# Two decoder blocks in split fp32: the down projections move into the braided stage's slots and banks

## The chip, the cores and the metric

The kernel runs on one core of one Trainium2 chip. The metric is device time in microseconds (us) for one execution, 2815.57 us as the median of 3 runs (2812.67 to 2816.57).

## The reference

Two transformer blocks run one after the other on 256 tokens of width 2048 in fp32. Cut to the matrix products:

```python
# first block
proj = rmsnorm(x) @ w_in                       # queries, keys, pool, gates
y_pool, y_attn = pool(proj) @ w_pool_o, attention(proj) @ w_attn_o
x = x + (g_pool * y_pool + g_attn * y_attn) @ w_out
h2 = rmsnorm(x)
x = x + (silu(h2 @ w_ffn_gate) * (h2 @ w_ffn_up)) @ w_ffn_down      # 2048 -> 5632 -> 2048
# second block
proj = rms_norm(x) @ w_in_2                    # stick-breaking attention, spatial gating
x = x + (sigmoid(ga) * y_a + sigmoid(gb) * y_b) @ w_out_2
h2 = rms_norm(x)
x = x + square(relu(h2 @ w_ff1_2)) @ w_ff2_2                        # 2048 -> 8192 -> 2048
```

## The kernel before

Every matrix product keeps fp32 accuracy by splitting each operand into a high part and a low part in `fp32r`: `x*w` is taken as `xh*wh + xh*wl + xl*wh`, three matmuls. The activations are stationary (128 x 128), the weights move (512 or 256 columns).

**Pieces.** The weights come in pieces of 512 KB. A piece is loaded by SyncE's DMA queue (SP) into a raw buffer (`R`, 4 buffers, or `G`, 3 buffers, for Strassen pieces). ScalarE (ACT) rounds it to the high part, a CAST (line L226). VectorE (DVE) subtracts to get the low part (L228). Both go into a slot of the tile `W`. Then TensorE (PE) multiplies. An ordinary piece is 1024 numbers wide and feeds 12 matmuls of 512 columns (L258 with the high part, L259 with the low part, L260 with the high part). A Strassen piece is four blocks of 256 columns, to which DVE first adds three sums (L203 to L205). It is 1792 wide when split and feeds 21 matmuls of 256 columns (L310 to L312).

**Kinds of piece.** There are three: `PLAIN`, `MIX` and `STR`. `W` has 13 x 1024 columns, and the kinds share them. A PLAIN piece takes one of six slots, 0 to 5. A MIX piece takes one of slots 0 to 2. A STR piece takes one of two wide slots that lie on the columns of PLAIN slots 3 to 5. So PLAIN slots meet the columns of both other kinds, and MIX and STR never meet. Slots of one kind are used in turn.

**Order.** All engines' instructions are written out in one order by `drive()`, which walks over a list of jobs. Before the matmuls of piece k it emits the splits of the pieces up to k + 4 (PLAIN) or k + 3 (MIX, STR), but only while the slot's last user has been emitted already (`free_h[...] <= used[0]`). Where that doesn't hold, this split and all behind it come later in the queues of ACT and DVE, behind whatever was emitted in between. Engines work their queues in order. On the chip a split also waits until the slot's last user has left PE.

**Stages.** The work around the change, for each of the two feed-forward parts:

- `wide(...)`: the product with `w_out` or `w_out_2`, four chunks of 512 columns with 8 PLAIN pieces each. After each chunk the sum into `X` (L860) and squares (L404) are taken, and one piece into the next chunk the result is transposed by PE (`transposed_s`, L352) and split for the next stage.
- the braided stage: `braid(...)` weaves a MIX chunk (gate, or an even chunk of `w_ff1_2`) with a Strassen chunk (up, or an odd chunk). The MIX chunk sums in banks 4 and 5 of PSUM, the Strassen chunk in banks 0 to 3. At the end of a braid `fin` of `strassen` reads banks 0 to 3 (ACT L323, DVE L324 to L327), and in the second block ACT then applies relu and square (L1182, L1183). The first block has 4, 4 and 3 braids in its three groups, the second block 2 braids in each of four groups.
- the down stage after each group: four chunks with `w_ffn_down` (8, 8 and 6 PLAIN pieces each) or `w_ff2_2` (8 each), into banks taken in turn from `FREE[PLAIN]`, 0 to 3. They are added to `X` by DVE (L896). Into the first of the four chunks the transposes of the last braid's result are put (`transposed`, PE L382, then ACT L369 and DVE L370 copy them out of PSUM). These use auxiliary banks: 4, 5, 6 and 7 in mode PLAIN, 6 and 7 in mode MIX. The second block transposes two chunks at once there (`two`), which takes four banks' worth.

`stage(MIX)` and `stage(PLAIN)` only set which auxiliary banks are used. There are three sorts of change of stage: from `wide` to the first braid, from the last braid of a group to the down stage, and from the down stage to the next group's first braid.

Of the kernel before, what the change touches and what calls it, by code (L numbers as in the profile page):

```python
# [17 lines left out]
NT = 2  # L18
D = 2048
KT = D // P  # L20
# [6 lines left out]
PLAIN, MIX, STR = 0, 1, 2  # L27
# [44 lines left out]
def body(tc, d, out):  # L72
# [4 lines left out]
    with tc.manual_schedule(), \  # L77
# [48 lines left out]

        mode = [PLAIN]
        naux = [0]
        FREE = {PLAIN: [0, 1, 2, 3], MIX: [4, 5]}
        AUX = {PLAIN: (4, 5, 6, 7), MIX: (6, 7)}  # L130

        def bank_at(b):
# [14 lines left out]
        def stage(m):  # L147
            run(lambda: mode.__setitem__(0, m))

        def hslots(kind, n):  # L150

            if kind == STR:
                return (n % 2) * 1792, (2 + n % 2) * 1792, 1792
            s = n % (3 if kind == MIX else 6)
            o = 7168 + 1024 * s if s < 3 else 1024 * (s - 3)
            return o, o + 3072, 1024

        def drive():
            pcs = [j for j in jobs if j[0] == "pc"]
# [2 lines left out]
            seen_h, seen_r, cnt = {}, {}, {}  # L162
            for i, j in enumerate(pcs):
                kind = j[5]
                n = cnt.get(kind, 0)
                cnt[kind] = n + 1
                num.append(n)
                a, b, w = hslots(kind, n)
                cells = [(o + x) // 256 for o in (a, b) for x in range(0, w, 256)]
                free_h.append(max(seen_h.get(x, -1) for x in cells))  # L170
                seen_h.update((x, i) for x in cells)
                rk = kind == STR
                m = cnt.get(("r", rk), 0)
# [34 lines left out]
            def split(upto):  # L208
                while ns[0] <= min(upto, len(pcs) - 1) and free_h[ns[0]] <= used[0]:
                    i = ns[0]  # L210
                    dma()
                    if i in before_split:
                        before_split[i]()
                    sums(i + 2)
                    kind = pcs[i][5]
                    a, b, w = hslots(kind, num[i])
# [42 lines left out]
            pe.matmul(o, x[0], w[1], start=False, stop=False)  # L259
            pe.matmul(o, x[1], w[0], start=False, stop=last)  # L260

        def chunk(pair, w, kts, c0, n, evict, row0=0, inject=None, kind=PLAIN):

            items, banks = [], []

            def mk(j):
                def fn(h, l):
                    if j == 0:
                        banks.extend([FREE[kind].pop(0) for _ in range(NT)])
                    for q in range(2):  # L270
                        kt = 2 * j + q
                        for tok in range(NT):
                            mm3(bank_at(banks[tok])[:, :n], pair(kt, tok), (h[:, q, :], l[:, q, :]), kt == 0, kt == kts - 1)
                return fn

            for j in range(kts // 2):
                if inject and j in inject:
                    items.append(("run", inject[j]))
                items.append(piece(wsrc(w, row0 + 2 * j, c0, n), mk(j), kind=kind))

            def fin():
                for tok in range(NT):
                    evict(tok, bank_at(banks[tok])[:, :n])
                FREE[kind].extend(banks)

            items.append(("run", fin))
            return items
# [542 lines left out]
        def wide(pair, w, ev, tr, pending, kts=16, inject=None, row0=0):  # L830

            for c in range(4):
                inj = dict(inject or {}) if c == 0 else {}
                if pending is not None:
                    at = 3 if c == 0 else 1
                    old, new = inj.get(at), pending
                    inj[at] = new if old is None else (lambda a=new, b=old: (a(), b()))
                jobs.extend(chunk(pair, w, kts, c * 512, 512, ev(c), inject=inj, row0=row0))
                pending = tr(c)
            return pending  # L840

# [33 lines left out]

        h2T = pairat(A, 0, KT)
        h2F = rview(C, 0, 2, KT // 2, 4, P)
        pending = wide(mixT, "w_out", ev_res(tmp, inv2), t_x(h2T, "ffn", h2F), pending)


        abuf = rview(G, 0, NT, 512)

        def ev_silu(tok, ps):
            act.activation(abuf[:, tok, :], ps, AF.Silu, scale=inv2[:, tok : tok + 1])
# [13 lines left out]

        inv3 = stat(2)
        hT = pairat(A, 0, KT)  # L900
        groups = [(0, 4), (4, 4), (8, 3)]
        for gi, (c0, nch) in enumerate(groups):
            aT = pairat(B, 0, 16)
            stage(MIX)
            for j in range(nch):
                c = c0 + j
                jobs.extend(braid(chunk(h2T, "w_ffn_gate", KT, c * 512, 512, ev_silu, kind=MIX),
                                  strassen(h2T, h2F, "w_ffn_up", KT, c * 512, ev_up),
                                  {4: pending} if pending is not None else None))
                pending = t_a(aT, blocks(abuf), j)  # L910
            stage(PLAIN)
            lastg = gi == len(groups) - 1
            for oc in range(4):
                inj = {}
# [1 line left out]
                    inj[nch * 2 - 4 if oc == 0 else 1] = pending  # L916
                    pending = None
                ev = ev_res(tmp, inv3)(oc) if lastg else ev_acc(oc)
                jobs.extend(chunk(aT, "w_ffn_down", 4 * nch, oc * 512, 512, ev, row0=4 * c0, inject=inj))
                if lastg:  # L920
                    pending = t_x(hT, "mix")(oc)


        w2 = "w_in_2"
# [250 lines left out]
            pending = t_mer(c)  # L1175

        inv4 = stat(2)
        pending = wide(merT, "w_out_2", ev_res(tmp, inv4), t_x(h2T, "ff", h2F), pending)


        def relu2(o, tok, v):
# [11 lines left out]
        def ev_out(c):  # L1193
# [3 lines left out]
                sync.dma_start(out[tok * P : (tok + 1) * P, c * 512 : (c + 1) * 512], xs)  # L1197
            return f

        for gi in range(4):  # L1200
            aT = pairat(B, 0, 16)
            stage(MIX)
            for j in range(0, 4, 2):
                c = 4 * gi + j
                jobs.extend(braid(chunk(h2T, "w_ff1_2", KT, c * 512, 512,
                                        lambda tok, ps: relu2(abuf[:, tok, :], tok, ps), kind=MIX),
                                  strassen(h2T, h2F, "w_ff1_2", KT, (c + 1) * 512, lambda tok, v: relu2(v, tok, v)),
                                  {4: pending} if pending is not None else None))
                pending = two(t_a(aT, blocks(abuf), j), t_a(aT, half, j + 1))
            stage(PLAIN)  # L1210
            for oc in range(4):
                inj = {}
                if pending is not None:
                    inj[4] = pending
                    pending = None
                ev = ev_out(oc) if gi == 3 else ev_acc(oc)
                jobs.extend(chunk(aT, "w_ff2_2", 16, oc * 512, 512, ev, row0=16 * gi, inject=inj))

        drive()

# [80 lines left out]
```

## Time and profile before

| what | value |
| --- | --- |
| median of 3 runs | 2815.57 us |
| the profiled execution's own time | 2811.55 us |
| its span, first to last instruction | 2809.8 us |
| PE busy | 2743.7 us, 98% |
| DVE busy | 1853.1 us, 66% |
| ACT busy | 1402.6 us, 50% |
| mean granted clock of PE | 0.988 |

PE is the engine that sets the time. Its idle time is small, and where it lies is seen in the view of waits and in stretches cut out around the changes of stage. The granted clock is 1.0 (2.4 GHz) or 0.5 (1.2 GHz); a stretch's mean says how much of it ran at the lower level.

### The profile page before, as it was taken

To read this page: it belongs to the slowest core of one execution; us is meant where nothing else is said; L and a number is where in the kernel's file an instruction comes from. 1 tells how busy PE (TensorE), PEld (TensorE's weight loads), DVE (VectorE), ACT (ScalarE), POOL (GpSimd) and SP (SyncE) were. 2 spreads that over 40 slices of the span, in tenths; PEclk is the share of its full clock that TensorE was granted. 3 is DMA by queue.
4 is the path that set the end of the run, shared out by engine and by line. 5 is a ranking of instruction groups with operands and counts; after the bars stand their busy time and mean duration, and the time that the engine had idled before them with its cause. 6 is when DMAs were issued, how large, how long until landed. Compare 5 with 4: busy or idle time off the path is not lost. (4 is left out here: it accounts for less than half of the span.)

```text
span 2809.8 us, 35965 instructions
## 1 busy us (share of the span) xinstructions
PE 2743.7 (98%) x13996; PEld 2300.2 (82%) x13996; DVE 1853.1 (66%) x2233; ACT 1402.6 (50%) x1749; POOL 72.9 (3%) x153
## 2 busy tenths in 40 slices
PE   9999999999999999999999999999999989989989
PEld 8888888888888888888888888888787877878777
DVE  6554676767985798489655564555685675764763
ACT  6544666455554455355455555434454354453552
POOL 1000111000000000000010100000000000000000
PEclk9999999999999999999999999999999999999999
DMA  7656444555546555645554554555445536545444
GB/s 262 209 203 201 150 142 135 191 181 187 186 171 203 195 193 182 202 159 186 193 181 169 194 171 164 204 183 176 173 171 173 189 135 202 188 150 202 145 168 146
DMA packets 143179, 506.66 MB, mean 180 GB/s; under 512 B 16160, under 2 KB 18592, under 8 KB 142496
## 3 DMA queue, kind: packets, MB, share of 16 engines
q1 hardware_dynamic: 142864, 504.31, 52.1%
q8 instruction: 109, 1.79, 0.2%
q14 instruction: 62, 0.51, 0.1%
q10 hardware_dynamic: 144, 0.05, 0.0%
HBM read 502.21 MB, written 2.10 MB: 179 GB/s over the span
## 5 line engine op out<-in xcount | busy, mean ns | idle before, releaser
L228 DVE TENSOR_TENSOR W<-R,W 128x1024 fp32r<-128x1024 f32 (+2 forms) x795 | 938.6, 1206 | 431.6 <-ACT W L226 428.8
L226 ACT CAST W<-R 128x1024 fp32r<-128x1024 f32 (+2 forms) x798 | 807.9, 1036 | 522.2 <-PE PS L260 341.1
L258 PE MATMUL PS<-W,A 128*128 128x512 f32 (+2 forms) x1728 | 682.1, 395 | 10.1 <-ACT W L226 10.1
L259 PE MATMUL PS<-W,A 128*128 128x512 f32 (+2 forms) x1728 | 682.4, 395 | 9.0 <-DVE W L228 9.0
L260 PE MATMUL PS<-W,A 128*128 128x512 f32 (+2 forms) x1728 | 680.0, 393 | 0.0
L258 PE MATMUL PS<-W,B 128*128 128x512 f32 (+1 forms) x1248 | 496.3, 398 | 21.9 <-DVE tmp L326 15.1
L259 PE MATMUL PS<-W,B 128*128 128x512 f32 (+1 forms) x1248 | 493.7, 396 | 3.9 <-DVE W L228 3.9
L260 PE MATMUL PS<-W,B 128*128 128x512 f32 (+1 forms) x1248 | 493.5, 395 | 0.0
L226 ACT CAST W<-G 128x1792 fp32r<-128x1792 f32 x152 | 257.3, 1693 | 340.5 <-PE PS L311 153.0
L259 PEld LDWEIGHTS PS<-W,A 128*128 128x128 f32 x1728 | 326.7, 189 | 81.0 <-DVE W L228 14.2
L258 PEld LDWEIGHTS PS<-W,A 128*128 128x128 f32 x1728 | 326.6, 189 | 80.0 <-ACT W L226 12.3
L260 PEld LDWEIGHTS PS<-W,A 128*128 128x128 f32 x1728 | 326.3, 189 | 74.2
L228 DVE TENSOR_TENSOR W<-G,W 128x1792 fp32r<-128x1792 f32 x152 | 307.0, 2020 | 57.4 <-ACT W L226 57.3
L258 PEld LDWEIGHTS PS<-W,B 128*128 128x128 f32 x1248 | 236.5, 190 | 78.4 <-ACT W L226 12.2
L259 PEld LDWEIGHTS PS<-W,B 128*128 128x128 f32 x1248 | 236.5, 189 | 59.4 <-DVE W L228 5.7
L260 PEld LDWEIGHTS PS<-W,B 128*128 128x128 f32 x1248 | 236.3, 189 | 55.3 <-DVE B L370 0.4
L310 PE MATMUL PS<-W,C 128*128 128x256 f32 x608 | 170.7, 281 | 0.0
L312 PE MATMUL PS<-W,C 128*128 128x256 f32 x608 | 170.6, 281 | 0.0
L311 PE MATMUL PS<-W,C 128*128 128x256 f32 x608 | 170.3, 280 | 0.0
L310 PE MATMUL PS<-W,A 128*128 128x256 f32 x456 | 130.6, 286 | 0.0
L312 PE MATMUL PS<-W,A 128*128 128x256 f32 x456 | 128.4, 281 | 0.4 <-DVE W L228 0.4
L311 PE MATMUL PS<-W,A 128*128 128x256 f32 x456 | 128.4, 282 | 0.0
(231 smaller groups left out, 2496.5 us busy)
## 6 DMA issues: line engine op xcount, KB each, us to landing
R<-in_w_in_dram SPq DMA_DIRECT2D x224, 512.0 KB, 4.5
R<-in_w_ff_dram SPq DMA_DIRECT2D x192, 512.0 KB, 4.4
R<-in_w_ffn_gate_dram SPq DMA_DIRECT2D x88, 512.0 KB, 4.4
G<-in_w_ffn_up_dram SPq DMA_DIRECT2D x88, 512.0 KB, 3.5
R<-in_w_ffn_down_dram SPq DMA_DIRECT2D x88, 512.0 KB, 4.3
R<-in_w_out_dram SPq DMA_DIRECT2D x64, 512.0 KB, 4.3
G<-in_w_ff_dram SPq DMA_DIRECT2D x64, 512.0 KB, 3.6
R<-in_w_attn_o_dram SPq DMA_DIRECT2D x32, 512.0 KB, 4.3
```

The lines of the kernel that those rows point to most:

```text
L226: act.copy(hv, v)
L228: dve.tensor_tensor(lv, v, hv.bitcast(F32), op=ALU.subtract)
L258: pe.matmul(o, x[0], w[0], start=first, stop=False)
L259: pe.matmul(o, x[0], w[1], start=False, stop=False)
L260: pe.matmul(o, x[1], w[0], start=False, stop=last)
L310: pe.matmul(o, xh, h[:, wi, :], start=first, stop=False, skip_group_check=True)
L311: pe.matmul(o, xl, h[:, wi, :], start=False, stop=False, skip_group_check=True)
L312: pe.matmul(o, xh, l[:, wi, :], start=False, stop=last, skip_group_check=True)
```

## The change

The down projections become MIX pieces, in slots 0 to 2 of `W`, and so does the last chunk of each `wide(...)`. Each slot is now chosen as the one of its kind whose columns were used longest ago. The down chunks sum in banks of their own list, `DOWN`: 4 and 5, then 0 and 1, 4 and 5, 2 and 3; the MIX chunk of a braid is fixed to 4 and 5 as it was. Mode MIX stays on through a whole feed-forward part, so the transposes in the down stage have banks 6 and 7 alone.

```diff
-        FREE = {PLAIN: [0, 1, 2, 3], MIX: [4, 5]}
+        FREE = [0, 1, 2, 3]
         AUX = {PLAIN: (4, 5, 6, 7), MIX: (6, 7)}
...
-        def hslots(kind, n):
-
-            if kind == STR:
-                return (n % 2) * 1792, (2 + n % 2) * 1792, 1792
-            s = n % (3 if kind == MIX else 6)
+        def hslots(s):
+
+
+            if s >= 6:
+                return (s - 6) * 1792, (s - 4) * 1792, 1792
             o = 7168 + 1024 * s if s < 3 else 1024 * (s - 3)
             return o, o + 3072, 1024
+
+        SLOTS = {PLAIN: range(6), MIX: range(3), STR: range(6, 8)}
...
-                n = cnt.get(kind, 0)
-                cnt[kind] = n + 1
-                num.append(n)
-                a, b, w = hslots(kind, n)
-                cells = [(o + x) // 256 for o in (a, b) for x in range(0, w, 256)]
-                free_h.append(max(seen_h.get(x, -1) for x in cells))
-                seen_h.update((x, i) for x in cells)
+
+                def cells(s):
+                    a, b, w = hslots(s)
+                    return [(o + x) // 256 for o in (a, b) for x in range(0, w, 256)]
+
+                last, s = min((max(seen_h.get(x, -1) for x in cells(s)), s) for s in SLOTS[kind])
+                num.append(s)
+                free_h.append(last)
+                seen_h.update((x, i) for x in cells(s))
...
-        def chunk(pair, w, kts, c0, n, evict, row0=0, inject=None, kind=PLAIN):
-
-            items, banks = [], []
+        def chunk(pair, w, kts, c0, n, evict, row0=0, inject=None, kind=PLAIN, fixed=None):
+
+            items, banks = [], list(fixed or ())
...
-                jobs.extend(chunk(pair, w, kts, c * 512, 512, ev(c), inject=inj, row0=row0))
+                jobs.extend(chunk(pair, w, kts, c * 512, 512, ev(c), inject=inj, row0=row0,
+                                  kind=last if c == 3 else PLAIN))
...
-        pending = wide(mixT, "w_out", ev_res(tmp, inv2), t_x(h2T, "ffn", h2F), pending)
+        pending = wide(mixT, "w_out", ev_res(tmp, inv2), t_x(h2T, "ffn", h2F), pending, last=MIX)
...
+        DOWN = [(4, 5), (0, 1), (4, 5), (2, 3)]
...
+        stage(MIX)
         groups = [(0, 4), (4, 4), (8, 3)]
         for gi, (c0, nch) in enumerate(groups):
             aT = pairat(B, 0, 16)
-            stage(MIX)
...
-            stage(PLAIN)
             lastg = gi == len(groups) - 1
...
-                jobs.extend(chunk(aT, "w_ffn_down", 4 * nch, oc * 512, 512, ev, row0=4 * c0, inject=inj))
+                jobs.extend(chunk(aT, "w_ffn_down", 4 * nch, oc * 512, 512, ev, row0=4 * c0, inject=inj,
+                                  kind=MIX, fixed=DOWN[oc]))
                 if lastg:
                     pending = t_x(hT, "mix")(oc)
+
+        stage(PLAIN)
```

The second block's loop over `w_ff1_2` and `w_ff2_2` is changed in the same way.

The order of instructions changes at three places. The first is ACT's queue at the end of the second group in the second block, where the last braid gives way to the down stage. Before, where L226 with 128x1024 splits an ordinary piece, L226 with 128x1792 a Strassen piece, and L369 copies the transposes:

```order
798 L226 CAST W<-G 128x1792 x2
799 L1182 ACTIVATE G<-PS,st 128x512
800 L1183 ACTIVATE G<-G 128x512
801 L1182 ACTIVATE G<-PS,st 128x512
802 L1183 ACTIVATE G<-G 128x512
803 L323 COPY tmp<-PS 128x256
804 L1182 ACTIVATE G<-G,st 128x2x256
805 L1183 ACTIVATE G<-G 128x2x256
806 L1182 ACTIVATE tmp<-tmp,st 128x512
807 L1183 ACTIVATE tmp<-tmp 128x512
808 L226 CAST W<-R 128x1024 x8
809 L369 CAST B<-PS 128x512 x4
```

And now, where every line number of `kernel.py` is a few higher (L230 for L226, L1191 for L1182, L328 for L323):

```order
803 L230 CAST W<-R 128x1024
804 L1191 ACTIVATE G<-PS,st 128x512
805 L1192 ACTIVATE G<-G 128x512
806 L1191 ACTIVATE G<-PS,st 128x512
807 L1192 ACTIVATE G<-G 128x512
808 L230 CAST W<-R 128x1024 x2
809 L328 COPY tmp<-PS 128x256
810 L1191 ACTIVATE G<-G,st 128x2x256
811 L1192 ACTIVATE G<-G 128x2x256
812 L1191 ACTIVATE tmp<-tmp,st 128x512
813 L1192 ACTIVATE tmp<-tmp 128x512
814 L230 CAST W<-R 128x1024 x3
```

Three splits of down pieces that stood behind the braid's last eviction now stand ahead of it, and the fourth is the first one behind it.

The second place is ACT's queue at the end of `w_out_2`, where L404 takes the squares of the last chunk. Before:

```order
704 L226 CAST W<-R 128x1024 x3
705 L404 ACTIVATE tmp,st<-X 128x512 x2
706 L226 CAST W<-R 128x1024 x2
707 L226 CAST W<-G 128x1792
708 L226 CAST W<-R 128x1024
```

And now:

```order
708 L230 CAST W<-R 128x1024 x7
709 L230 CAST W<-G 128x1792
710 L409 ACTIVATE tmp,st<-X 128x512 x2
711 L230 CAST W<-R 128x1024
712 L230 CAST W<-G 128x1792
```

The first two MIX pieces and the first Strassen piece of the braid are now split ahead of the last chunk's eviction, and splits of this chunk itself moved behind the transposes.

The third place is DVE's queue where the third down stage of the second block gives way to the fourth group. L896 evicts the last down chunk, L203 to L205 are the sums of a Strassen piece. Before:

```order
1464 L896 TENSOR_TENSOR X<-X,PS 128x512 x2
1465 L203 TENSOR_TENSOR G<-G 128x512
1466 L204 TENSOR_TENSOR G<-G 128x256
1467 L205 TENSOR_TENSOR G<-G 128x256
1468 L228 TENSOR_TENSOR W<-R,W 128x1024 x2
```

And now, where L903 is the eviction and L232 the low part:

```order
1469 L232 TENSOR_TENSOR W<-R,W 128x1024 x2
1470 L207 TENSOR_TENSOR G<-G 128x512
1471 L208 TENSOR_TENSOR G<-G 128x256
1472 L209 TENSOR_TENSOR G<-G 128x256
1473 L232 TENSOR_TENSOR W<-G,W 128x1792
1474 L903 TENSOR_TENSOR X<-X,PS 128x512 x2
```

Two MIX splits, the next sums and the first Strassen split moved ahead of the eviction.

## Rows read from the trace of the kernel before

**Rows 1.** The page, part 1: busy time and share of the span by engine.
```profile
PE 2743.7 (98%) x13996; PEld 2300.2 (82%) x13996; DVE 1853.1 (66%) x2233; ACT 1402.6 (50%) x1749; POOL 72.9 (3%) x153
```

**Rows 2.** The view of cores: span and mean granted clock.
```profile
core 0: 2809.8 us, clock 0.988
```

**Rows 3.** The view of waits, PE alone: us in total, times, longest.
```profile
PE PS L258 <- ACT W L226: 16.9, 10, 6.0
PE PS L382 <- DVE B L370: 15.1, 4, 4.9
PE PS L258 <- DVE tmp L326: 15.1, 6, 4.1
PE PS L259 <- DVE W L228: 12.9, 13, 2.4
```

**Rows 4.** Stretches: length, busy (count) of PE, PEld, DVE, ACT, POOL; PEclk; DMA.
```profile
830.00:860.00 30.00, 25.54 (x124) 21.13 (x124) 19.41 (x20) 13.56 (x16) 0.00 (x0) 0.89 0.45 152
1100.00:1120.00 20.00, 17.45 (x89) 14.72 (x88) 13.81 (x15) 8.90 (x10) 0.00 (x0) 0.91 0.60 206
1328.00:1345.00 17.00, 14.89 (x90) 12.93 (x89) 12.94 (x16) 8.23 (x11) 0.00 (x0) 1.00 0.43 144
2117.00:2137.00 20.00, 17.54 (x89) 14.34 (x88) 10.70 (x12) 11.28 (x16) 0.00 (x0) 0.91 0.40 131
2306.00:2330.00 24.00, 17.57 (x89) 14.49 (x88) 12.54 (x12) 14.32 (x18) 0.00 (x0) 0.86 0.30 106
2502.00:2525.00 23.00, 18.87 (x96) 15.90 (x95) 13.68 (x13) 14.43 (x18) 0.00 (x0) 0.93 0.39 137
2700.00:2725.00 25.00, 21.29 (x106) 17.32 (x105) 13.72 (x13) 14.95 (x18) 0.00 (x0) 0.93 0.38 130
2016.00:2036.00 20.00, 16.15 (x68) 12.72 (x68) 14.90 (x20) 9.25 (x11) 1.38 (x2) 0.83 0.28 99
1194.00:1214.00 20.00, 17.07 (x76) 13.62 (x75) 14.88 (x19) 8.79 (x7) 0.00 (x0) 0.91 0.26 88
2600.00:2620.00 20.00, 17.06 (x76) 13.65 (x75) 13.79 (x17) 7.69 (x7) 0.00 (x0) 0.91 0.22 79
2160.00:2200.00 40.00, 40.00 (x173) 32.10 (x173) 19.94 (x19) 15.04 (x15) 0.00 (x0) 1.00 0.56 180
```

**Rows 5.** Timeline, second down stage of the second block begins: start, us, what, [idle before].
```profile
2319.02 0.79 PE L258 MATMUL PS<-W,B 128*128 128x512 f32 x1 [5.96 <-ACT W L226]
```

**Rows 6.** Timeline, third down stage of the second block begins.
```profile
2506.35 2.93 ACT L226 CAST W<-R 128x1024 fp32r<-128x1024 f32 x3
...
2510.82 0.68 DVE L324 TENSOR_TENSOR G<-tmp,PS 128x512 f32<-128x512 f32 x1
...
2513.53 0.47 PE L258 MATMUL PS<-W,B 128*128 128x512 f32 x1 [4.13 <-DVE tmp L326]
...
2516.32 2.93 ACT L226 CAST W<-R 128x1024 fp32r<-128x1024 f32 x3
```

**Rows 7.** Timeline, transposes with two auxiliary banks, inside a braid of the second block.
```profile
2085.18 1.04 PE L382 MATMUL PS<-cst,G 128*128 128x128 f32 x8
...
2085.81 1.07 ACT L369 CAST B<-PS 128x512 fp32r<-128x512 f32 x2 [1.61 <-PE PS L382]
...
2088.87 1.28 DVE L370 TENSOR_TENSOR B<-PS,B 128x512 fp32r<-128x512 f32 x2
...
2089.61 0.33 PE L382 MATMUL PS<-cst,G 128*128 128x128 f32 x1 [3.40 <-DVE B L370]
```

**Rows 8.** Timeline, the last chunk of `w_out_2`: its transposes, and splits behind them.
```profile
2000.03 1.03 PE L352 MATMUL PS<-cst,X 128*128 128x128 f32 x8
...
2006.08 3.49 DVE L228 TENSOR_TENSOR W<-R,W 128x1024 fp32r<-128x1024 f32 x3
```

**Rows 9.** Timeline, second down stage of the first block ends.
```profile
1198.87 1.38 DVE L896 TENSOR_TENSOR X<-X,PS 128x512 f32<-128x512 f32 x2 [13.80 <-PE PS L260]
...
1202.96 0.50 PE L259 MATMUL PS<-W,A 128*128 128x512 f32 x1 [1.80 <-DVE W L228]
```

More of the change, by code (lines that the diff above doesn't have):

```diff
@@ L215, in split @@
                     kind = pcs[i][5]
-                    a, b, w = hslots(kind, num[i])
+                    a, b, w = hslots(num[i])
                     h, l = W[:, a : a + w], W[:, b : b + w]
@@ L260, in mm3 @@
             pe.matmul(o, x[1], w[0], start=False, stop=last)
-        def chunk(pair, w, kts, c0, n, evict, row0=0, inject=None, kind=PLAIN):
-            items, banks = [], []
+        def chunk(pair, w, kts, c0, n, evict, row0=0, inject=None, kind=PLAIN, fixed=None):
+            items, banks = [], list(fixed or ())
             def mk(j):
                 def fn(h, l):
-                    if j == 0:
-                        banks.extend([FREE[kind].pop(0) for _ in range(NT)])
+                    if j == 0 and not fixed:
+                        banks.extend([FREE.pop(0) for _ in range(NT)])
                     for q in range(2):
@@ L283, in fin @@
                     evict(tok, bank_at(banks[tok])[:, :n])
-                FREE[kind].extend(banks)
+                if not fixed:
+                    FREE.extend(banks)
             items.append(("run", fin))
@@ L828, in t_mix, with wide @@
                                       mixT, list(range(4 * c, 4 * c + 4)))
-        def wide(pair, w, ev, tr, pending, kts=16, inject=None, row0=0):
+        def wide(pair, w, ev, tr, pending, kts=16, inject=None, row0=0, last=PLAIN):
             for c in range(4):
@@ L903, in body @@
             aT = pairat(B, 0, 16)
-            stage(MIX)
             for j in range(nch):
                 c = c0 + j
-                jobs.extend(braid(chunk(h2T, "w_ffn_gate", KT, c * 512, 512, ev_silu, kind=MIX),
+                jobs.extend(braid(chunk(h2T, "w_ffn_gate", KT, c * 512, 512, ev_silu, kind=MIX, fixed=(4, 5)),
                                   strassen(h2T, h2F, "w_ffn_up", KT, c * 512, ev_up),
@@ L1177, in body @@
         inv4 = stat(2)
-        pending = wide(merT, "w_out_2", ev_res(tmp, inv4), t_x(h2T, "ff", h2F), pending)
+        pending = wide(merT, "w_out_2", ev_res(tmp, inv4), t_x(h2T, "ff", h2F), pending, last=MIX)
         def relu2(o, tok, v):
@@ L1198, in ev_out @@
             return f
+        stage(MIX)
         for gi in range(4):
             aT = pairat(B, 0, 16)
-            stage(MIX)
             for j in range(0, 4, 2):
@@ L1205, in body @@
                 jobs.extend(braid(chunk(h2T, "w_ff1_2", KT, c * 512, 512,
-                                        lambda tok, ps: relu2(abuf[:, tok, :], tok, ps), kind=MIX),
+                                        lambda tok, ps: relu2(abuf[:, tok, :], tok, ps), kind=MIX, fixed=(4, 5)),
                                   strassen(h2T, h2F, "w_ff1_2", KT, (c + 1) * 512, lambda tok, v: relu2(v, tok, v)),
@@ L1209, in body @@
                 pending = two(t_a(aT, blocks(abuf), j), t_a(aT, half, j + 1))
-            stage(PLAIN)
             for oc in range(4):
@@ L1216, in body @@
                 ev = ev_out(oc) if gi == 3 else ev_acc(oc)
-                jobs.extend(chunk(aT, "w_ff2_2", 16, oc * 512, 512, ev, row0=16 * gi, inject=inj))
+                jobs.extend(chunk(aT, "w_ff2_2", 16, oc * 512, 512, ev, row0=16 * gi, inject=inj,
+                                  kind=MIX, fixed=DOWN[oc]))
         drive()
```

## The prediction

> **What bounds the kernel now.** I read the busy times first: PE works 98% of the span, DVE 66%, ACT half [rows 1]. Only what lets PE run on without a break, or at a higher clock, can shorten the time. The view of waits says what is to be had: four kinds of wait make up 60.0 us of PE's idle time [rows 3]. The view of cores adds the clock: a mean of 0.988 over 2809.8 us means 33.7 us lost to the lower level, 1.2 GHz for 2.4 [rows 2]. More than about 93 us can't be gained by any change of order.
>
> Then I cut stretches out of the trace. Away from the changes of stage, in the middle of a down stage, PE is busy 40.00 us of 40.00 at the full clock, with 173 matmuls; so a matmul of 512 columns takes about 0.233 us and an ordinary piece of 12 about 2.80 us [rows 4]. At ten of the changes of stage PE has idle time, length less busy. The first seven stretches begin a down stage after a braid: 4.46, 2.55, 2.11, 2.46, 6.43, 4.13 and 3.71 us, together 25.85. The eighth begins the first braid after `w_out_2`: 3.85. The next two begin a braid after a down stage: 2.93 and 2.94 [rows 4]. That is 35.6 us. The rest of the idle time lies between two braids of one group in the second block, where the transposes alone wait 15.1 us for their banks [rows 3], and at the start; the change does not go there.
>
> The lower clock follows the idle time. In nine of the ten stretches the mean clock is 0.83 to 0.93, and it is 1.00 in the quiet one and in one with a gap of 2.11 us [rows 4]. Length times (1 - clock) is what the low level costs if PE has work meanwhile: 3.3, 1.8, 0, 1.8, 3.4, 1.6 and 1.8 us for the seven, 3.4 for the eighth, 1.8 and 1.8 for the last two, together 20.7 us.
>
> **The change, part by part.**
>
> *Braid to down.* Two things hold PE there. One is the banks: the first down chunk sums in banks that the Strassen eviction still reads, so PE waits for L326; this is six waits, 15.1 us [rows 3]. The other is the split: a PLAIN slot lies on Strassen columns, so the first splits stand behind the braid's last eviction, and PE waits 5.96 us for a CAST [rows 5]. Both go. Banks 4 and 5 were last read by the eviction of the MIX chunk, two Strassen pieces earlier, and the first three splits now stand ahead of the Strassen eviction, as the first piece of order shows. Their cover is these two Strassen pieces. Gain: 25.85 us idle and 13.7 us of clock, 39.5 us.
>
> What is late next is the fourth down piece, whose split is the first behind the eviction. The third group shows nearly that order already, with three CASTs (2.93 us) ahead of it: the eviction begins at 2510.82, the next CAST at 2516.32 [rows 6]. This CAST takes about 1.0 and the subtraction about 1.2 us, so the low part is there at 2518.6. With the wait gone PE would begin the stage at 2513.53 - 4.13 = 2509.40 and reach the second matmul of the fourth piece at 2509.40 + 3 x 2.80 + 0.23 = 2518.0. It is up to 0.6 us late. One of the three CASTs now runs before the MIX eviction, in time in which ACT would wait for PE, so the chain comes up to 0.5 earlier: I take 0.1, four times in the second block, 0.4 us; bounds 0 and 2.4. In the first block the eviction ends on DVE and not on ACT, and there is room.
>
> *Down to braid, and `w_out_2` to braid.* PE waits for CAST and subtraction of the first MIX piece, and DVE puts three sums in between; at 1202.96 it waits 1.80 us for the low part [rows 9]. Now two MIX pieces and the first Strassen piece are split ahead of the eviction, as the second and third piece of order show, during a stage in which DVE and ACT are half idle: 19.9 and 15.0 us of 40 [rows 4]. The eviction moves behind this: two MIX pieces' time, 5.6 us, covers it before the first Strassen matmul needs banks 2 and 3. Gain: 3.85 + 3.4 and 2.93 + 1.8 + 2.94 + 1.8, together 16.7 us.
>
> These gains add up to 56.2 us. Part of the low clock lies in idle time and is counted twice; I take off 0.7, so 55.5.
>
> *Three slots for six.* Inside the down stages a split now runs two pieces ahead of PE and not four. Its price is nothing as long as two pieces, 5.6 us, cover the chain after a slot comes free. At a chunk's end this is the eviction of 1.38 us [rows 9] and then about 1.2 for the subtraction, 2.7 with the steps between them; ACT's CAST runs beside the eviction. Without that cover it would be 2.7 us at each of 28 chunk ends. In the last chunk of `wide` it does not quite do: behind the transposes at 2000.03 the first subtraction ends at about 2006.08 + 1.2 = 2007.3 [rows 8]. This was a piece needed much later; now it is the fourth of the chunk. PE is back at matmuls by about 2000.9, takes two pieces and wants that low part at 2000.9 + 5.6 + 0.2 = 2006.7. Cost 0.6 us, in both blocks, 1.2.
>
> *Two auxiliary banks for four.* In the second block's down stage four banks' worth of transposes are put in at the fifth piece. Now the third must wait until the first has been copied out. A braid does the same thing already: the eight transposes take 1.04 us, ACT's copy begins 0.63 after them, takes about 0.55, DVE's about 0.64, and the next transposes begin at once when that is done, but DVE comes late there and PE waits 3.40 us [rows 7]. In the down stage DVE has no Strassen split before it, so the copy is through 0.63 + 0.55 + 0.64 + 0.1 = 1.9 us after the start, 0.9 us after the first eight; the fourth bank adds some 0.3. I take 1.2, four times, 4.8 us; bounds 0.9 and 3.4 each.
>
> The Trainium skill (Perfetto Trace Analysis, Optimization Strategy) speaks against both of these edits: a gap that keeps coming back on the engine that should be saturated can mean too few buffers in SBUF or PSUM. The trace agrees for the two banks [rows 7]; for the slots the quiet stretch shows no gap with six [rows 4], and with three no run here shows it. By that rule the down stages would get a gap at each chunk, and the time would be that of the last rival below, about 2836 us; by the rows it is 2766.
>
> No DMA, split or matmul is added. The raw buffers on SP's queue stay four, and their loads are emitted in the same order.
>
> **Sum.** 55.5 - 0.4 - 1.2 - 4.8 = 49.1 us. From the profiled execution's 2811.55 this makes 2762.4. That execution is 4.0 us under the median of the runs, 2815.57, so I forecast 2815.57 - 49.1, about 2766 us.
>
> **The rivals.**
>
> *The fourth piece is late, and the clock falls for it.* The full 0.6 us and a fall of 1.8 us [rows 4] at four places: 9.6 in place of 0.4, about 2775 us. For it: the eviction chain is that long [rows 6]. Against: the gap is small, and every stretch with a low clock has 2.46 us of idle time or more.
>
> *The transposes wait as in a braid.* 3.4 us and a fall of the clock, four times: 20.8 in place of 4.8, about 2782 us. With the clock alone it is 2773. For it: all four braids with two banks show such a wait, 15.1 us [rows 3]. Against: DVE has half its time free in the down stage.
>
> *The change does half of what it says*: raw loads or DVE are late at the changes, and splits that stand earlier in the queue run no earlier. Half of 55.5 is lost: about 2794 us. Against: DVE waits for ACT or PE at these places, not the reverse.
>
> *Slower: three slots are too few.* A stall at every chunk end, 12 in the first block and 16 in the second. It decides when it takes 49.1 / 28 = 1.75 us each, that is when the chain of 2.7 us grows beyond 5.6 + 1.75 = 7.4 us; with a fall of the clock behind each, 1.8 us, hardly more than the fall is needed. At 2.5 us each the time would be about 2836. Against: the chain is less than half of its cover.
>
> **How the numbers follow.** The likeliest 0.60; late fourth piece 0.13; transposes 0.15; half 0.07; slower 0.03; a little better than forecast, with nothing new late, 0.02. The range of 2755 to 2785 takes in the first three and the last of these: its low end is 2815.57 - 56.2, nothing new late, less the 3.9 us by which the three runs differ. A measurement of this kernel can tell 0.2%, 5.6 us, from no change; the chances of faster, same and slower are 0.95, 0.02 and 0.03.
>
> **What would show it.** In the changed kernel's waits the line for L326 is gone, the CAST's 16.9 us falls to about 5 (four waits between braids), the transposes' 15.1 rises to about 19, and the mean clock is near 0.995. Right after each braid the down stage's first matmul follows the last Strassen matmul. The fourth piece's low part, the transposes after it, and the fourth piece of the last `wide` chunk are where a new wait would stand. It is wrong if gaps appear at each chunk's end, or if the clock still falls at the changes of stage.

## The result, and the profile after

The changed kernel takes 2765.66 us (median of 4 runs, 2764.56 to 2767.39) against 2816.03 (4 runs, 2812.67 to 2816.57): a ratio of 0.9824, 95% interval 0.9807 to 0.9841. The forecast was 2766, with a range of 2755 to 2785. The profiled execution took 2765.54 us.

The page, part 1, and the view of cores of the changed kernel, to be read against [rows 1, 2]:

```profile
PE 2722.0 (98%) x13996; PEld 2285.7 (83%) x13996; DVE 1854.9 (67%) x2233; ACT 1404.2 (51%) x1749; POOL 72.8 (3%) x153
```

```profile
core 0: 2763.8 us, clock 0.997
```

No engine does less: the same 13996 matmuls. PE's busy time falls by 21.7 us, since less of it lies at the low clock: about 2763.8 x 0.003 = 8.3 us are now lost to that, where it was 33.7.

The view of waits, PE alone, to be read against [rows 3] (L226 is now L230, L228 is L232, L258 and L259 are L262 and L263, L326 is L331, L382 and L370 are L387 and L375):

```profile
PE PS L387 <- DVE B L375: 23.7, 8, 5.0
PE PS L263 <- DVE W L232: 6.1, 9, 0.8
PE PS L262 <- ACT W L230: 5.4, 5, 1.2
PE PS L422 <- POOL nh L417: 1.0, 1, 1.0
PE PS L317 <- DVE W L232: 0.8, 2, 0.4
PE PS L262 <- DVE X L866: 0.2, 1, 0.2
```

The wait for the Strassen eviction (L326, 15.1 us) has no line any more. The wait for a CAST fell from 16.9 to 5.4 us, four times 1.2 of it between two braids. The transposes' wait rose from 15.1 to 23.7 us. Stretches at the same places as [rows 4], in the columns given there:

```profile
830.00:860.00 30.00, 30.00 (x156) 25.23 (x155) 19.01 (x20) 14.37 (x16) 0.00 (x0) 1.00 0.52 164
...
2098.00:2118.00 20.00, 19.04 (x112) 16.19 (x111) 12.35 (x15) 12.36 (x19) 0.00 (x0) 1.00 0.48 158
2286.00:2310.00 24.00, 23.04 (x128) 19.37 (x127) 14.94 (x17) 13.99 (x20) 0.00 (x0) 1.00 0.43 144
...
2017.00:2037.00 20.00, 18.90 (x122) 16.74 (x121) 19.69 (x26) 12.22 (x14) 0.00 (x0) 1.00 0.48 169
1184.00:1204.00 20.00, 20.00 (x109) 17.03 (x108) 18.09 (x23) 10.47 (x9) 0.00 (x0) 1.00 0.60 219
```

The nine changes between braids and down stages that [rows 4] shows have no idle time left of their own, and the full clock. The 0.96 us in each of the second block's down stages are the transposes; the 1.10 us after `w_out_2` are two small new waits, 0.71 for the low part of the first braid's second MIX piece and 0.39 for a Strassen low part. Rows of the timeline where the first down stage of the second block begins (start, us, what, idle before):

```profile
2100.21 1.98 ACT L230 CAST W<-R 128x1024 fp32r<-128x1024 f32 x2
2102.09 0.36 ACT L328 COPY tmp<-PS 128x256 f32<-128x256 f32 x1
2102.74 0.40 PE L262 MATMUL PS<-W,B 128*128 128x512 f32 x1
2108.68 1.99 ACT L230 CAST W<-R 128x1024 fp32r<-128x1024 f32 x2
2109.75 2.36 DVE L232 TENSOR_TENSOR W<-R,W 128x1024 fp32r<-128x1024 f32 x2 [3.68 <-ACT W L230]
2115.20 1.29 DVE L375 TENSOR_TENSOR B<-PS,B 128x512 fp32r<-128x512 f32 x2 [1.55 <-ACT B L374]
2115.94 0.33 PE L387 MATMUL PS<-cst,G 128*128 128x128 f32 x1 [0.96 <-DVE B L375]
```

PE goes from the last Strassen matmul to the first down matmul at 2102.74 without a gap. The fourth piece's CAST begins at 2108.68, behind the eviction; its low part is there at 2109.75 + 1.2, about 2111.0, and PE wants it at 2102.74 + 3 x 2.80 + 0.23 = 2111.4. It is in time by 0.4 us. In the third of these stages the low part comes 0.4 us later, and there PE is 0.1 us late.

**Where the time came from.** For each place I took by how much PE's matmuls start later than at its quiet pace (0.2333 us for 512 columns and 0.109 for a transpose, worked out from the starts of the matmuls); this "excess" holds idle time and low clock together and counts nothing twice.

| place | before | after | change | forecast |
| --- | --- | --- | --- | --- |
| seven changes from braid to down | 39.3 | 0 | -39.3 | -39.5 |
| `w_out_2` to braid, two changes from down to braid | 16.8 | 1.6 | -15.2 | -16.7 |
| counted twice in the forecast | | | | +0.7 |
| fourth down piece | 0 | 0.1 | +0.1 | +0.4 |
| last wide chunk, both blocks, and first block's first braid | 0.7 | 3.1 | +2.4 | +1.2 |
| transposes in the second block's down stages | 0 | 5.4 | +5.4 | +4.8 |
| gaps and transposes between two braids | 38.1 | 37.4 | -0.7 | 0 |
| start, and the second block's beginning | 2.4 | 3.8 | +1.4 | 0 |
| sum | | | -45.9 | -49.1 |

The two profiled executions differ by 46.0 us (2811.55 and 2765.54), which the places add up to; the medians differ by 50.4. The profiled execution of the kernel before is one of its quicker ones: in a later set its nine runs were 2811.5 to 2811.9 (four, clock 0.988 or 0.989) and 2815.9 to 2817.3 (five, clock 0.986).

### The profile page after: what moved, and what is told of

Read it like the earlier page. It is cut to its first block, busy times and chain, and to the rows that moved or that the text cites. A ratio compares the mean times of both kernels' runs of the same rounds, so it can differ in the third digit from the quotient of the medians.

```text
span 2763.8 us, 35989 instructions
## 1 busy us (share of the span) xinstructions
PE 2722.0 (98%) x13996; PEld 2285.7 (83%) x13996; DVE 1854.9 (67%) x2233; ACT 1404.2 (51%) x1749; POOL 72.8 (3%) x153
## 5 line engine op out<-in xcount | busy, mean ns | idle before, releaser
L232 DVE TENSOR_TENSOR W<-R,W 128x1024 fp32r<-128x1024 f32 (+2 forms) x795 | 943.2, 1208 | 527.6 <-ACT W L230 525.0
L230 ACT CAST W<-R 128x1024 fp32r<-128x1024 f32 (+2 forms) x798 | 810.0, 1035 | 533.2 <-PE PS L264 439.6
L262 PE MATMUL PS<-W,A 128*128 128x512 f32 (+2 forms) x1728 | 678.6, 393 | 5.6 <-ACT W L230 5.4
L263 PE MATMUL PS<-W,A 128*128 128x512 f32 (+2 forms) x1728 | 678.8, 393 | 5.2 <-DVE W L232 5.2
L262 PE MATMUL PS<-W,B 128*128 128x512 f32 (+1 forms) x1248 | 491.7, 394 | 0.0
L263 PE MATMUL PS<-W,B 128*128 128x512 f32 (+1 forms) x1248 | 489.5, 392 | 0.9 <-DVE W L232 0.9
L230 ACT CAST W<-G 128x1792 fp32r<-128x1792 f32 x152 | 257.3, 1693 | 316.3 <-PE PS L316 155.3
L263 PEld LDWEIGHTS PS<-W,A 128*128 128x128 f32 x1728 | 324.7, 188 | 75.5 <-DVE W L232 9.2
L262 PEld LDWEIGHTS PS<-W,A 128*128 128x128 f32 x1728 | 324.5, 188 | 74.1 <-ACT W L230 6.3
L232 DVE TENSOR_TENSOR W<-G,W 128x1792 fp32r<-128x1792 f32 x152 | 307.1, 2020 | 53.4 <-ACT W L230 53.4
L263 PEld LDWEIGHTS PS<-W,B 128*128 128x128 f32 x1248 | 234.1, 188 | 55.1 <-DVE W L232 2.1
L264 PEld LDWEIGHTS PS<-W,B 128*128 128x128 f32 x1248 | 233.9, 187 | 54.1
L262 PEld LDWEIGHTS PS<-W,B 128*128 128x128 f32 x1248 | 234.0, 188 | 53.9
```

Of the source, the lines that this page charges most:

```text
L262: pe.matmul(o, x[0], w[0], start=first, stop=False)
```

## The experiments

Each was timed beside the kernel before on one chip, not always the same; there the kernel before had medians of 2815.8 to 2817.0.

**The slots alone.** Banks and auxiliary banks as before, slots as changed:

```diff
+            stage(MIX)
...
+            stage(PLAIN)
             for oc in range(4):
...
-                                  kind=MIX, fixed=DOWN[oc]))
+                                  kind=MIX))
```

> The change with the down chunks back in banks 0 to 3 and with four auxiliary banks in the down stages. My theory: the splits still run ahead, but PE waits again for the Strassen eviction (L326 before) at each of the seven changes from braid to down, 2.1 to 3.0 us each, since three splits now stand ahead of that eviction on DVE, with falls of the clock of up to 1.8 us behind some; the transposes in the down stages don't wait, 1.3 us less at four places. About 2766 + 18 + 6 - 5 = 2785 us (2775 to 2792). The rival, that the splits were all that held PE and the bank wait is hidden once they are early: about 2761 us and no such wait.

Measured: 2788.99 us (2787.45 to 2790.27), ratio 0.9903 (0.9889 to 0.9918). From its waits:

```profile
PE PS L262 <- DVE tmp L331: 18.6, 7, 3.3
PE PS L387 <- DVE B L375: 16.6, 4, 4.9
```

The first line is the Strassen eviction at all seven changes from braid to down (2.1 us in the first block, about 3 in the second), and the low clock follows each. Down stages have no transposes' wait. The slots without the banks are worth 28 us of the 50; the rest needs the banks.

**The choice of slot alone.** The kernel before, in which each slot is the one used longest ago; no piece changes its kind, no bank changes:

```diff
-                n = cnt.get(kind, 0)
-                cnt[kind] = n + 1
-                num.append(n)
...
+                last, s = min((max(seen_h.get(x, -1) for x in cells(s)), s) for s in SLOTS[kind])
+                num.append(s)
```

> The kernel before with one edit: a piece takes the slot of its kind that was used longest ago. Banks and kinds are as before. My theory: the splits run ahead as in the change, and only the waits for the Strassen eviction stay, as in the run with slots only: about 2785 us (2775 to 2794). The rival, that the kind MIX is needed: the waits for the CAST at the changes stay too, 2800 to 2815 us.

Measured: 2783.58 us (2782.5 to 2786.93), ratio 0.9886 (0.9872 to 0.9901). From its waits (L330 is the eviction):

```profile
PE PS L262 <- DVE tmp L330: 18.6, 7, 3.3
PE PS L386 <- DVE B L374: 13.6, 4, 3.4
PE PS L262 <- ACT W L230: 5.4, 5, 1.2
```

The CAST's 16.9 us are 5.4 already, so down pieces need not be MIX for their splits to run ahead of the changes. With six PLAIN slots taken in turn, the next one often lies on Strassen columns that are still in use; the one used longest ago does not. Some two thirds of the change's gain, 33 of 50 us, can be had by this one rule. The opposite case, down pieces as MIX with their slots taken in turn, was not run. As slots 0 to 2 share no column with the Strassen slots, the rule by which `drive()` orders the splits would let them run as far ahead as in the changed kernel. So either edit seems to be enough for the splits; the run shows it for the choice of slot.

**Choice of slot and banks**, with the down chunks and the last `wide` chunk PLAIN:

```diff
-        pending = wide(mixT, "w_out", ev_res(tmp, inv2), t_x(h2T, "ffn", h2F), pending, last=MIX)
+        pending = wide(mixT, "w_out", ev_res(tmp, inv2), t_x(h2T, "ffn", h2F), pending)
...
-                                  kind=MIX, fixed=DOWN[oc]))
+                                  fixed=DOWN[oc]))
...
```

> The change, but down pieces and the last chunk of the wide products stay PLAIN, with six slots; the choice of the slot used longest ago, the fixed banks and the two auxiliary banks stay. My theory after reading the order: it is the choice of slot, not the kind, that lets the splits run ahead, since even a PLAIN piece then takes a slot that no Strassen piece has just used. So 2764 to 2767 us, as the change, without the 0.46 us in the last wide chunk and with no wait at the changes of stage. The rival, that slots apart from the Strassen columns are needed, as the change's own words say: waits of about 2.9 us and a fall of the clock come back at the first braids of groups, five places, 2775 to 2790 us.

Measured: 2776.68 us (2774.6 to 2778.46), ratio 0.9862 (0.9846 to 0.9879). No wait of more than 0.4 us stands at any change of stage, as expected, but the time is 10 us above the expectation. Rows of the timeline at the transposes of the first down stage show why:

```profile
2109.07 1.03 PE L387 MATMUL PS<-cst,G 128*128 128x128 f32 x8
2109.60 1.05 ACT L230 CAST W<-R 128x1024 fp32r<-128x1024 f32 x1 [1.91 <-DMA R<-in_w_ff_dram]
2110.55 1.07 ACT L374 CAST B<-PS 128x512 fp32r<-128x512 f32 x2
2110.68 1.23 DVE L232 TENSOR_TENSOR W<-R,W 128x1024 fp32r<-128x1024 f32 x1 [1.17 <-ACT W L230]
2111.82 1.28 DVE L375 TENSOR_TENSOR B<-PS,B 128x512 fp32r<-128x512 f32 x2
2112.56 0.33 PE L387 MATMUL PS<-cst,G 128*128 128x128 f32 x1 [2.46 <-DVE B L375]
```

Behind the eviction five splits stand ahead of the transposes' copies in both queues, and not three as in the changed kernel. The fifth waits for its load on SP's queue, and the copies wait behind it. PE waits 2.46 us in place of 0.96, in the other three stages 2.57, 2.82 and 3.40, and behind these three the clock falls. Three slots hold the last two back. So this is what the MIX kind adds to the choice of slot and the banks: 11 us, by doing less ahead.

**Two slots.** The down chunks in slots 0 and 1 only:

```diff
-        SLOTS = {PLAIN: range(6), MIX: range(3), STR: range(6, 8)}
+        SLOTS = {PLAIN: range(6), MIX: range(3), STR: range(6, 8), TWO: range(2)}
...
-                                  kind=MIX, fixed=DOWN[oc]))
+                                  kind=TWO, fixed=DOWN[oc]))
```

> The change with two slots in place of three for the down pieces. It asks where the cover of the shorter lead ends. My theory: inside a chunk nothing is lost, since CAST and subtraction take 2.4 us of the 2.8 of the one piece that is left as cover. Lost are the third down piece after each braid, whose split then stands behind the eviction, about 2.6 us and a fall of the clock of 1.8 in the second block (four places) and 0.6 in the first (three), about 1 us at each chunk end of the first block's last group, and 0 to 0.3 us at the other chunk ends: 2785 to 2795 us. The rival, that too few buffers make a gap at every chunk or piece: 2836 us or more.

Measured: 2780.79 us (2777.91 to 2781.4), ratio 0.9873 (0.9858 to 0.9887), below the expected range. From its waits:

```profile
PE PS L263 <- DVE W L232: 11.9, 17, 0.9
PE PS L262 <- ACT W L230: 8.0, 12, 1.2
```

The third piece of the second block's down stages comes 1.14 us late (four times), and chunk ends wait 1.2 us in the first block's last group alone, three times. None at the others: one piece of cover, 2.80 us, is enough there. The late third piece cost less than expected, 1.14 us in place of 2.6, and the clock does not fall behind it. The prediction's slower rival, that three slots are too few, was further away than it had reckoned: even two make no gap at most chunk ends.

**The transposes' halves apart**, at two places in a braid and two in a down chunk:

```diff
-                                  {4: pending} if pending is not None else None))
-                pending = two(t_a(aT, blocks(abuf), j), t_a(aT, half, j + 1))
+                                  {4: pending} if callable(pending) else dict(zip((4, 7), pending or ()))))
+                pending = (t_a(aT, blocks(abuf), j), t_a(aT, half, j + 1))
...
-                    inj[4] = pending
+                    inj[4], inj[5] = pending
```

> The changed kernel, but the two halves of the second block's double transposes are put in at two places and not at one: in a braid ahead of the fifth and the eighth piece, in a down stage ahead of the fifth and the sixth. The banks stay 6 and 7. First theory: in the down stage the two banks alone make PE wait, 0.96 us of idle time and an excess of 1.63 us over PE's pace, four times, so this goes (about 6 us); inside the braids the wait of 4.95 us goes over to PE's waiting for the Strassen split, which DVE does late in any case, so only about 1 us each is won: about 2757 us (2752 to 2763). Rival: inside the braids too it is only the banks that hold PE; then four waits of 4.95 us and the low clock behind them go as well: about 2733 us.

Measured: 2737.56 us (2736.09 to 2739.37), ratio 0.9724 (0.9708 to 0.9741). The rival was right in its mechanism, though 4 us too low: L387 has no line left among the waits, and only a small new one (L374) stands in the down chunk behind it. From its waits:

```profile
PE PS L263 <- DVE W L232: 6.1, 9, 0.8
PE PS L262 <- ACT W L230: 5.3, 5, 1.2
PE PS L422 <- POOL nh L417: 1.0, 1, 1.0
PE PS L262 <- ACT B L374: 1.0, 4, 0.2
```

My error shows in rows of the changed kernel's timeline between two braids:

```profile
2059.15 0.51 PE L262 MATMUL PS<-W,A 128*128 128x512 f32 x1 [1.18 <-ACT W L230]
2060.41 0.50 PE L263 MATMUL PS<-W,A 128*128 128x512 f32 x1 [0.76 <-DVE W L232]
2061.80 2.02 DVE L232 TENSOR_TENSOR W<-G,W 128x1792 fp32r<-128x1792 f32 x1
2063.07 1.03 PE L387 MATMUL PS<-cst,G 128*128 128x128 f32 x8
2066.39 2.02 DVE L232 TENSOR_TENSOR W<-G,W 128x1792 fp32r<-128x1792 f32 x1
2068.32 1.28 DVE L375 TENSOR_TENSOR B<-PS,B 128x512 fp32r<-128x512 f32 x2
2069.06 0.41 PE L387 MATMUL PS<-cst,G 128*128 128x128 f32 x1 [4.96 <-DVE B L375]
```

I had taken the split that ends at 2068.41 for the one that PE wants right behind the transposes. That is the one before it, which ends at 2063.82. DVE is late, but not for anything that PE needs then, except the two banks.

**Strassen pieces four ahead**, to use the 3.7 us in which DVE waits at that place:

```diff
-AHEAD = {PLAIN: 4, MIX: 3, STR: 3}
+AHEAD = {PLAIN: 4, MIX: 3, STR: 4}
```

> The changed kernel, but a Strassen piece's splits run four pieces ahead and not three, so that the next braid's second ordinary piece is rounded ahead of the Strassen eviction. Theory: the waits between two braids of a group (1.18 and 0.76 us, then 4.95 us for the transposes, four times) come from DVE standing idle 3.7 us behind a CAST that is queued behind that eviction; with this CAST ahead, DVE comes through earlier, most of the three waits go, and the low clock behind them with it: about 2746 us (2738 to 2756). Rival: DVE has as much to do in either order and the wait only moves: 2766 us.

Measured: 2772.61 us (2771.64 to 2773.75), ratio 0.9848 (0.9834 to 0.9863): the theory fell, and the rival was still too kind. From its waits:

```profile
PE PS L387 <- DVE B L375: 25.5, 8, 5.4
PE PS L315 <- DVE tmp L331: 12.6, 12, 1.1
```

The 1.18 and 0.76 us are gone, but the extra split now stands ahead of the Strassen eviction on DVE, and the next braid's first Strassen matmul waits 1.05 us for banks 0 to 3. This happens four times in the second block, and eight times in the first, which had no wait there at all. The transposes wait 5.4 us in place of 4.95.

**Both edits together.**

> The edits of the last two together. If the transposes' wait between braids has its root in DVE's late start, the two add up: 2766 - 9 - 20, about 2737 us (2728 to 2746). If banks alone held PE the first edit would have taken it all and this run is within 3 us of that one.

Measured: 2739.67 us (2739.2 to 2740.42), ratio 0.9732 (0.9717 to 0.9746). Within 3 us of the halves apart alone, as the rival says. The time by itself decides nothing, as the theory had forecast it too, but it had counted on 9 us from the first edit and 20 from the second; alone, the first brought 28 and the second cost 7. The banks had been the whole of the transposes' wait.

**Four auxiliary banks in the second block's down stages** (6, 7, 2 and 3), all else as changed:

```diff
-        AUX = {PLAIN: (4, 5, 6, 7), MIX: (6, 7)}
+        AUX = {PLAIN: (4, 5, 6, 7), MIX: (6, 7), STR: (6, 7, 2, 3)}
...
-                    inj[4] = pending
+                    inj[4] = lambda p=pending: (mode.__setitem__(0, STR), p(), mode.__setitem__(0, MIX))
```

> The changed kernel, but the double transposes of the second block's down stage alone have four auxiliary banks again: 6, 7, 2 and 3 (the last two are free until the fourth chunk). Theory: this is the term of the sum for two auxiliary banks by itself. The wait in the down stages (0.96 us idle, excess over pace 1.63 us, four times) goes: 2766 - 6.5, about 2759 us (2756 to 2763). Rival: the wait there is for DVE and ACT and not for the banks, and PE then waits for the transposed operand's low part: no change, 2766 us.

Measured: 2760.86 us (2756.83 to 2763.85), ratio 0.9806 (0.9791 to 0.982). Of the transposes' eight waits the four between braids are left:

```profile
PE PS L387 <- DVE B L375: 16.7, 4, 4.9
```

The first down stage takes 91.11 us from its first to its last matmul and 92.46 in the changed kernel, so two banks cost 1.35 us a stage, 5.4 in all; the 1.63 of the expectation was 0.28 too high. The medians differ by 4.8 us. The term for two auxiliary banks is real and is a matter of banks.

**PLAIN slots and four banks**: the run with choice of slot and banks, with this last edit.

> The changed kernel with the down projections and the last wide chunk back in the six ordinary slots (that is the run with the choice of slot and the banks alone, 2776.7 us) and with four auxiliary banks for the double transposes of the second block's down stages (6, 7, 2 and 3). Theory: the braided stage's slots help only because they keep splits from standing in front of the transposes' copies while there are two banks; with four banks nothing waits there, the excess of 3.13, 4.87, 5.03 and 6.82 us at these four places goes, and the time is 2776.7 - 19.9, about 2757 us (2753 to 2762), no slower than the changed kernel with four banks (2760.9 us). Rival: the ordinary slots delay something else in the down stages too, such as the low part of the transposed operand; then it is above 2765 us.

Measured: 2763.98 us (2762.4 to 2766.57), ratio 0.9818 (0.9805 to 0.9832): between theory and rival, just below the rival's 2765. Two new lines among its waits:

```profile
PE PS L264 <- DVE B L375: 2.6, 4, 0.7
PE PS L262 <- ACT B L374: 2.5, 4, 1.2
```

The late copies no longer hold banks, but the next matmuls wait for the transposed operand itself, 0.9 to 1.8 us at each place where it was 2.5 to 3.4: 5.1 us in all in place of 11.3. So a little over half of that waiting was for the banks, and the rest for the operand. The 3 us to the run before lie within the intervals, so with four banks it is not shown that three slots beat six.

**Halves apart in the braids, four banks in the down stages.**

> The changed kernel with the transposes' halves apart inside the second block's braids alone (2738 us with halves apart in both places), and four auxiliary banks for the double transposes of its down stages. If the two waits are separate, each is gone: the down stages lose the 0.82 us of excess that the split halves left there, four times, so 2738 - 3.3, about 2734 us (2731 to 2738). If halves apart in the braids only push DVE's work on into the down stages, their transposes wait again by 1 us or more each, and it is 2740 us or above.

Measured: 2737.21 us (2735.99 to 2739.73), ratio 0.9727 (0.9713 to 0.974). The waits in the down stages are gone as expected, and yet the time is that of the halves apart. Stretches at three of the four gaps between braids:

```profile
2059.00:2062.00 3.00, 2.04 (x8) 1.45 (x9) 2.74 (x5) 2.70 (x3) 0.00 (x0) 1.00 0.00 0
2239.00:2246.00 7.00, 6.24 (x27) 4.97 (x28) 6.86 (x9) 5.05 (x6) 0.00 (x0) 0.76 0.17 57
2420.00:2427.00 7.00, 6.04 (x24) 4.81 (x25) 6.72 (x8) 5.06 (x6) 0.00 (x0) 0.76 0.13 39
```

The same 1.9 us of idle time is followed by the full clock once and by the low one three times, where the run with halves apart in both places had one such fall in its profile: two falls more, at about 1.5 us, took back about what the down stages gained.

**The best version**: that kernel, with the last `wide` chunk PLAIN again and Strassen pieces four ahead in the second block alone.

```diff
-        pending = wide(merT, "w_out_2", ev_res(tmp, inv4), t_x(h2T, "ff", h2F), pending, last=MIX)
+        pending = wide(merT, "w_out_2", ev_res(tmp, inv4), t_x(h2T, "ff", h2F), pending)
...
+        run(lambda: ahead.__setitem__(STR, 4))
         for gi in range(4):
```

> The last run's kernel, and with it two more edits: the last chunk of each wide product keeps ordinary slots, as before the change (that part of the change then only cost, 1.65 us in each block by the traces, so -3.3), and Strassen pieces run four ahead in the second block alone (2.47 us of excess at the gap between two braids becomes 1.29 + 0.33, four times, -3.4; the first block, where this cost 1.29 us at eight places, keeps three). Expected 2734 - 6.7, about 2727 us (2723 to 2732). If the last chunk's slots were needed for the change to work where the braids begin, a wait of some 3.9 us stands there again in each block, with the low clock behind it, and it is 2738 us or above.

Measured: 2726.63 us (2726.16 to 2727.3), ratio 0.9689 (0.9676 to 0.9702). The view of cores, and from its waits:

```profile
core 0: 2724.8 us, clock 0.999
```

```profile
PE PS L316 <- DVE tmp L332: 4.3, 4, 1.1
PE PS L264 <- DVE W L233: 1.5, 2, 0.8
```

No wait of more than 1.2 us is left behind the start, the clock does not fall behind any of them, and the runs lie within 1.2 us of each other. The MIX slots in the last `wide` chunk bought nothing that the choice of slot did not bring: the run with choice of slot and banks has no more than a wait of 0.4 us at that change either.

## Why the prediction was right, step by step

- **Braid to down** (39.5 forecast, 39.3 measured). Both causes were named rightly: with earlier splits alone, 18.6 us of waiting for the eviction stay, and they go with the banks. No run has the banks alone. What the prediction left open is that down pieces need not be MIX for it: with PLAIN pieces, the choice of slot and the banks no wait stands at these changes either. Length times (1 - clock) over a stretch was a good price for the clock.
- **Down to braid and `w_out_2` to braid** (16.7 forecast, 15.2 measured). From down to braid nothing is left; at `w_out_2` two waits of 0.71 and 0.39 us took a part back. This term was off by most, 1.5 us.
- **Fourth down piece** (0.4 forecast, 0.1 measured). From the stage's first matmul to the low part the prediction had read 9.2 us off the rows and allowed for up to 0.5 less. It took 8.2 us in three stages and 8.6 in the third, where PE wants it at 8.6. The rival that rests on it did not happen, with little room to spare in that stage.
- **Three slots** (1.2 forecast, 2.4 measured). The fourth piece of the last `wide` chunk waits 0.46 us in each block, an excess of 0.73, so 1.5 in all. Not foreseen: the first braid's second MIX piece comes 0.7 us late, an excess of 0.95 in each block. Both are gone in the run where that chunk is PLAIN. No chunk end of a down stage waits.
- **Two auxiliary banks** (4.8 forecast, 5.4 measured). The copy is through 1.9 us after the start, as worked out, and PE idles 0.96 us; 0.39 more is lost as the second half of the transposes runs below pace. The Trainium skill (Perfetto Trace Analysis, Optimization Strategy) says that a gap that keeps coming back can mean too little SBUF or PSUM. For the banks the trace agrees: four equal gaps of 0.96 us, gone with four banks. For the slots it doesn't: six in place of three made the transposes' gaps longer, 2.46 to 3.40 us.
- **The transposes' line**: forecast about 19, measured 23.7. Between braids it rose from 15.1 to 19.8 us, four times 4.95. Before, the low clock had slowed PE behind the 1.94 us gap at three of these four places, and DVE caught up meanwhile, so PE waited only 3.4 us. The excess there is nearly the same, 38.1 and 37.4. A run shows both cases side by side: in the one with four auxiliary banks two places have a fall and waits of 3.39 and 3.41 us, and two have none and waits of 4.94.
- **The sum.** The number came out closer than its working. Of the 3.2 us that are missing from the 49.1, the gains were 1.0 smaller and the costs 1.5 larger than forecast, and 0.7 lay where none was forecast. 2766 was reached because I set the sum against the median of before, 4 us above its profiled run; against the profiled run it would have been 2762.4, 3 us too low. That these two errors nearly cancel is luck; that each term came out near its size is not.

What stays open: why the same gap is followed by the low clock in one execution and not in another.

## What to carry to other kernels

Where splits stop short of a change of stage, look at which slot the next piece takes before giving it more or other slots: here one rule, the slot used longest ago, made two thirds of the gain by itself. Running further ahead is not better in itself: on queues that work in order, each split that runs ahead stands in front of some copy or eviction. Three slots beat six by 11 us for that reason while the transposes had two banks, and three Strassen pieces ahead beat four by 7 us. It has to be read from the trace place by place: in the best version four pieces ahead stand in the second block, where they turn a gap of 1.9 us into one of 1.1. Ask of each late instruction which resource PE wants from it then; moving half of the transposes was worth 28 us, and the engine that was late got no faster for it.

## What the hardware showed that I had not expected

Between two braids the same gap of 1.91 to 1.95 us, in two waits with one matmul between them, stands four times in each of ten kernels (before, after and eight experiments). Behind 22 of these 40 the granted clock fell to 0.5 (1.2 GHz) for a time, and behind 18 it did not. Behind no wait of 1.3 us or less that stood alone did it fall in any of the thirteen profiles, the start and the end of the span apart.

What a fall costs depends on what PE waits for next. In eight of the ten kernels the transposes' wait follows, and the excess up to the end of that wait is 7.66 us with a fall and without, in all 32 cases: the slower matmuls only take the place of waiting. In the two kernels with the halves apart nothing follows, and the excess is 4.0 to 4.1 us behind the four gaps with a fall and 2.5 behind the four without. So a wait cut from 1.9 to 1.1 us could give back more than its length in the best version, where the excess is 1.5 to 1.6 us at each of these places.

Only one execution of each kernel has a profile, so it is not shown that these gaps are also why executions of one kernel differ, by up to 7 us with four auxiliary banks (mean clock 0.992 to 0.996) and by 1 us in the best version (0.999 in each).
